# A decoder layer on one core: three tile pairs from plain to seven products, one of four opening pieces in one pass, the last column half in a bank of its own

## The chip, the cores and the metric

The kernel runs on one core of a Trainium2 chip. The metric is the device time of one execution in microseconds (us); less is better.

## The reference

One decoder layer, 512 tokens of 1024 features in float32, and three steps, each with a residual and a layer norm:

```python
def swiglu(x, w_gate, w_up, w_down):
    return (jax.nn.silu(x @ w_gate) * (x @ w_up)) @ w_down      # 1024 -> 2816 -> 1024
...
x = layer_norm(ALPHA * x + 0.5 * swiglu(x, ffn1_w_gate[l], ffn1_w_up[l], ffn1_w_down[l]), ln1_g[l], ln1_b[l])
proj = x @ w_in[l]                                               # 1024 -> 3072
...                                                              # gated recurrence (4 heads) and causal conv
mix = jnp.concatenate([o_a, o_b], axis=-1) @ w_out[l]
x = layer_norm(ALPHA * x + mix, ln2_g[l], ln2_b[l])
x = layer_norm(ALPHA * x + 0.5 * swiglu(x, ffn2_w_gate[l], ffn2_w_up[l], ffn2_w_down[l]), ln3_g[l], ln3_b[l])
```

## The kernel before

Every float32 operand of a product is split into a high and a low part (`split`): ScalarE casts the high part (L68), VectorE, or GpSimd for some weights of the mixing step, subtracts it from the raw value (L76). A product is then three matmuls, high by high, high by low and low by high (`mm3`, L194 to L196).

**Gate and up products.** The 2816 hidden columns of an FFN are 11 tile pairs f of 2 x 128 columns. For each there is a gate quad (s = 0) and an up quad (s = 1) of weights, one DMA of 1 MB each. A quad is taken in one of two ways. `plain` streams 512 tokens: 2 column tiles x 8 row tiles x 3 = 48 matmuls of 512 columns. `seven` cuts tokens, rows and columns in halves and needs seven half products instead of eight (`SEVEN`, `product`, L414): 7 x 4 x 3 = 84 matmuls of 256 columns, in the order p7, p1, p4, p5, p2, p6, p3. For it VectorE forms sums of weight quarters (L143, L149, L150) and splits three and a half 1024-element pieces instead of two; for the tokens it forms `x.sums()` (s1, s2, s3) and later `last_sum()` (s4). p4 adds into the PSUM area of p7, so ScalarE has to copy p7 out first (L434). The first `PLAIN` = 2 pairs of each FFN are plain, the other nine seven.

**Two seams.** The down product and the output product are made by `rows_out`: for the second half of the columns the last four weight units are kept, and the four token tiles are finished one after the other. Each is added to the residual (L333), its statistics taken (L334, L339), normalized (L221 and L343 on VectorE, the power on GpSimd at L222, then L347), transposed on TensorE (eight matmuls, L274 or L288), cast by ScalarE and its low part made by VectorE (L278 or L291). To keep TensorE busy while the last two tiles are normalized, the first four column products of the next step (`four_halved` before the mixing step, `begin` before the second FFN) run in token halves, t = 0 for tokens 0 to 255 first. They are 4 x 24 matmuls of 256 columns for t = 0, then as many for t = 1, which needs the transposes of the last tiles. `NORM_WAITS` says how much of this goes ahead of the transposes of tile 2 and of tile 3. The last tile's last unit is taken in two column halves of 256, both in one PSUM bank.

**Order.** TensorE's order is that of the code (`manual_schedule`); a scheduler orders the other engines. Each engine runs its queue in that order. The parts of weights lie in 6 slots (`parts`), the raw weights in 2 buffers (`raws`).

Of the kernel before, what the change touches and what calls it, by code (L numbers as in the profile page):

```python
# [17 lines left out]
P = 128  # L18
# [8 lines left out]
PLAIN = 2  # L27
# [22 lines left out]
NORM_WAITS = (1.3, 6.2)  # L50
# [3 lines left out]
def decoder_layer(ctx, tc, x_tok, x_q, w_first, vec, bcast, ng, w_gu1, w_d1, w_i, w_g, w_col, w_o, w_gu2, w_d2, out):  # L54
# [115 lines left out]
    def plan_quads(src, first):  # L170
        todo.extend(("plain" if f < PLAIN else "seven", src[f, s]) for f in range(first, NP) for s in range(2))

# [8 lines left out]
    plan_quads(w_gu1, 1)  # L181
# [8 lines left out]
    plan_quads(w_gu2, 0)  # L190
# [122 lines left out]
    def rows_out(ks, per, lhs, accs, factor, late, finish, follow=(), before=lambda u: None, then=lambda: None):  # L313
# [4 lines left out]
        n_units = len(ks) // per  # L318

        wide = [512] * (NT - 1) + [256]  # L320
        stats = [small.tile([P, 1024 // n, 6], F32, tag=f"stats{n}", name="stats") for n in wide]

        def part(acc, u, hi, lo, i, cols=slice(0, 512)):
            for j in range(per):
                n = per * u + j
                h, l = lhs(ks[n])
                mm3(acc[i][:, cols], h[:, i * P:(i + 1) * P], l[:, i * P:(i + 1) * P],
                    hi[:, j, cols], lo[:, j, cols], n == 0, n == len(ks) - 1, skip_group_check=wide[i] < 512)

        def add(acc, half, i, c):  # L330
            n = wide[i]
            z = xres[i][:, half * 512 + c:half * 512 + c + n]
            nc.vector.scalar_tensor_tensor(z, acc[i][:, c:c + n], factor, z, op0=ALU.mult, op1=ALU.add)  # L333
            nc.vector.bn_stats(stats[i][:, (half * 512 + c) // n, :], z)  # L334
# [16 lines left out]
        with tc.manual_schedule(engines={PE}):  # L351
            for u in range(n_units):
                before(u)
                hi, lo = unit()
                for i in range(NT):
                    part(acc, u, hi, lo, i)
        for i in range(NT):
            for c in range(0, 512, wide[i]):
                add(acc, 0, i, c)
        acc = [bank(b) for b in accs[1]]  # L360
        for u in range(n_units - late):
            hi, lo = unit()
            for i in range(NT):
                part(acc, u, hi, lo, i)
# [4 lines left out]
        with tc.manual_schedule(engines={PE}):  # L369
            left = deque()  # L370
            for i in range(NT):
                for n, (u, hi, lo) in enumerate(kept[:-1]):
                    part(acc, u, hi, lo, i)
# [6 lines left out]
                for c in range(0, 512, wide[i]):  # L380
                    add(acc, 1, i, c)
# [9 lines left out]
    def four_halved(pp, banks):  # L391
# [677 lines left out]
```

## Time and profile before

| | |
|---|---|
| median of 3 runs | 935.68 us (934.78 to 935.89) |
| profiled execution | 935.08 us, its span 933.1 us, 1.98 us around it |
| mean granted TensorE clock | 0.998 |
| TensorE (PE) busy | 923.2 us, 99% of the span |
| VectorE (DVE), ScalarE (ACT), GpSimd (POOL) busy | 72%, 41%, 13% |

A matmul's record is longer than its distance to the next, since matmuls are pipelined: what one costs in a dense stretch is the distance from start to start. Times in the rows are us from the start of the span.

### The profile page before, as it was taken

Reading aid. Unit: us, or ns where it says so; the run is one execution under the profiler, and the core shown is the slowest. Engines: PE = TensorE matmul, PEld = TensorE weight load, DVE = VectorE, ACT = ScalarE, POOL = GpSimd, SP = SyncE. Lnnn points to the kernel's source line nnn. Section 1 sums busy time; section 2 is a strip of 40 time slices with the busy share of each in tenths; the row PEclk is TensorE's granted clock in tenths of the full one; section 3 lists DMA queues with packets and bytes.
Section 4 is the critical chain, followed back from the end, with each engine's and each line's share of the span. In section 5 each row is a group of like instructions: output and inputs, shape, how many; then the busy total and the mean of one; then the engine's idle time right before and its main releaser. Section 6 shows DMA issues by size and latency. Waiting matters only on the chain.

```text
span 933.1 us, 14256 instructions
## 1 busy us (share of the span) xinstructions
PE 923.2 (99%) x5899; PEld 836.8 (90%) x5899; DVE 673.8 (72%) x953; ACT 384.1 (41%) x564; POOL 120.8 (13%) x142
## 2 busy tenths in 40 slices
PE   9999999999999999999999999999999999999996
PEld 6899999999888889888888888989999999988885
DVE  6978888887724265998898769948888887842317
ACT  5555445456412114414342714534545545721100
POOL 0000000000820014643462201000000000000001
PEclk9999999999999999999999999999999999999999
DMA  8522332324432212422130251122232222443302
GB/s 295 201 94 91 112 115 91 124 81 147 140 109 91 91 45 92 136 68 68 51 108 23 73 199 67 70 91 91 92 120 107 91 96 98 146 136 92 111 1 90
DMA packets 22464, 96.67 MB, mean 104 GB/s; under 512 B 2496, under 2 KB 3648, under 8 KB 17024
## 3 DMA queue, kind: packets, MB, share of 16 engines
q1 hardware_dynamic: 22320, 95.50, 30.6%
q8 instruction: 46, 0.75, 0.3%
q0 software_dynamic: 80, 0.26, 0.1%
q14 instruction: 18, 0.15, 0.1%
HBM read 93.66 MB, written 2.10 MB: 103 GB/s over the span
## 4 chain that ended last, share of the span: by engine, by line
PE 90%; DVE 4%; issue 3%; POOL 2%; DMA 1%; ACT 1%; DVEq 0%; POOLq 0%; ACTq 0%
PE bank L414 39%; PE bank L194 16%; PE bank L196 16%; PE bank L195 16%; DVE bank L771 2%; PE bank L849 1%; POOL wlo L76 1%; PE bank L274 0%; PE bank L288 0%; DMA raw<-w_g 0%; DMA xr<-x_q 0%; DVE diag L798 0%; DVE bl L954 0%; DVE m L906 0%; PE bank L920 0%
## 5 line engine op out<-in xcount | busy, mean ns | idle before, releaser
L68 ACT CAST whi<-raw 128x1024 fp32r<-128x1024 f32 (+2 forms) x172 | 172.9, 1010 | 307.3 <-PE bank L196 145.9
L76 DVE TENSOR_TENSOR wlo<-raw,whi 128x1024 fp32r<-128x1024 f32 (+2 forms) x150 | 173.4, 1164 | 174.1 <-ACT whi L68 174.0
L194 PE MATMUL bank<-whi,hp 128*128 128x512 f32 x324 | 125.9, 389 | 0.0
L196 PE MATMUL bank<-whi,hp 128*128 128x512 f32 x324 | 125.6, 388 | 0.0
L195 PE MATMUL bank<-wlo,hp 128*128 128x512 f32 x324 | 125.5, 387 | 0.0
L414 PE MATMUL bank<-ah,whi 128*128 128x256 f32 x432 | 122.5, 283 | 0.0
L414 PE MATMUL bank<-bl,whi 128*128 128x256 f32 x432 | 122.3, 283 | 0.0
L414 PE MATMUL bank<-ah,wlo 128*128 128x256 f32 x432 | 122.2, 283 | 0.0
L414 PE MATMUL bank<-al,whi 128*128 128x256 f32 x432 | 122.2, 283 | 0.0
L414 PE MATMUL bank<-bh,whi 128*128 128x256 f32 x432 | 122.2, 283 | 0.0
L414 PE MATMUL bank<-bh,wlo 128*128 128x256 f32 x432 | 122.2, 283 | 0.0
L771 DVE SCALAR_TENSOR_TENSOR bank<-u,vecs,bank 128x512 f32<-128x512 f32 x120 | 81.5, 750 | 3.8 <-ACT bank L766 3.6
L414 PEld LDWEIGHTS bank<-ah,whi 128*128 128x128 f32 x432 | 82.9, 192 | 0.2
L414 PEld LDWEIGHTS bank<-bh,whi 128*128 128x128 f32 x432 | 82.9, 192 | 0.1
L414 PEld LDWEIGHTS bank<-bl,whi 128*128 128x128 f32 x432 | 82.9, 192 | 0.1
L414 PEld LDWEIGHTS bank<-bh,wlo 128*128 128x128 f32 x432 | 82.9, 192 | 0.0
L414 PEld LDWEIGHTS bank<-al,whi 128*128 128x128 f32 x432 | 82.9, 192 | 0.0
L414 PEld LDWEIGHTS bank<-ah,wlo 128*128 128x128 f32 x432 | 82.9, 192 | 0.0
L222 POOL TENSOR_TENSOR rstd<-rstd,negh 128x1 f32<-128x1 f32 (+1 forms) x18 | 16.8, 935 | 509.4 <-DVE rstd L221 509.4
L76 POOL TENSOR_TENSOR wlo<-raw,whi 128x256 fp32r<-128x256 f32 x88 | 69.4, 821 | 61.1 <-ACT whi L68 59.1
L196 PEld LDWEIGHTS bank<-whi,hp 128*128 128x128 f32 x324 | 60.9, 188 | 12.8
L195 PEld LDWEIGHTS bank<-wlo,hp 128*128 128x128 f32 x324 | 60.9, 188 | 12.7
(210 smaller groups left out, 1911.2 us busy)
## 6 DMA issues: line engine op xcount, KB each, us to landing
raw<-w_gu SPq DMA_DIRECT2D x42, 1024.0 KB, 4.8
raw<-w_d SPq DMA_DIRECT2D x44, 512.0 KB, 3.5
raw<-w_col SPq DMA_DIRECT2D x16, 512.0 KB, 3.5
raw<-w_o SPq DMA_DIRECT2D x8, 512.0 KB, 3.5
xres<-x_tok SPq DMA_DIRECT2D x4, 512.0 KB, 7.8
gb<-bcast SPq DMA_DIRECT2D x4, 512.0 KB, 4.5
raw<-w_i SPq DMA_DIRECT2D x4, 512.0 KB, 3.4
raw<-w_g SPq DMA_DIRECT2D x4, 512.0 KB, 3.3
```

Of the source, the lines that this page charges most:

```text
L68: nc.scalar.copy(hi, raw)
L76: engine.tensor_tensor(lo[..., sl], raw[..., sl], hi.bitcast(F32)[..., sl], op=ALU.subtract)
L194: nc.tensor.matmul(ps, lhsT=lh, rhs=rh, start=first, stop=False, **kw)
L195: nc.tensor.matmul(ps, lhsT=lh, rhs=rl, start=False, stop=False, **kw)
L196: nc.tensor.matmul(ps, lhsT=ll, rhs=rh, start=False, stop=last, **kw)
L222: nc.gpsimd.tensor_tensor(r, r, negh.broadcast_to([P, n]) if n > 1 else negh, op=ALU.pow)
L414: nc.tensor.matmul(ps, lhsT=l[:, k, :], rhs=r[:, k, :], start=first and k == 0 and j == 0, stop=k == 3 and j == 2, skip_group_check=True)
L771: nc.vector.scalar_tensor_tensor(accs[n], us[n][:, j:j + T], vecs[:, w:w + 1], accs[n], op0=ALU.mult, op1=ALU.add)
L849: nc.tensor.matmul(ps[0:P - m, g, 0:64].rearrange("p (b m) -> p b m", m=m), lhsT=k[:, h, g * P:(g + 1) * P - m], rhs=halved(q, m, 1)[:, h, ...
```

## The change

1. `PLAIN` becomes a set of (f, s) for each FFN: `PLAINS`. In the first FFN the up quad of pair 1, in the second FFN the gate and the up quad of pair 1 are made with seven products. `last_sum` follows the first seven product, wherever it is.
2. In `four_halved` and `begin` the fourth piece is no longer cut in token halves: it runs whole, after the t = 1 halves of the other three. `NORM_WAITS` goes from 1.3 to 1.2.
3. In `rows_out` the last tile's last column half of 256 goes to the bank of the tile before it, as an accumulation of its own; what the older bank holds of these columns is added to the residual separately.

```diff
-PLAIN = 2
+PLAINS = ((0, 0), (0, 1), (1, 0)), ((0, 0), (0, 1))
...
-NORM_WAITS = (1.3, 6.2)
+NORM_WAITS = (1.2, 6.2)
...
-        todo.extend(("plain" if f < PLAIN else "seven", src[f, s]) for f in range(first, NP) for s in range(2))
+        todo.extend(("plain" if (f, s) in plain else "seven", src[f, s]) for f in range(first, NP) for s in range(2))
...
-                for c in range(0, 512, wide[i]):
-                    part(acc, *kept[-1], i, slice(c, c + wide[i]))
-                if i == NT - 1:
+                if i < NT - 1:
+                    add(acc[i], i, 512, 1024)
+                else:
+                    part(acc[i][:, 0:256], *kept[-1], i, slice(0, 256))
+                    add(acc[i][:, 256:512], i, 768, 1024, False)
+                    add(acc[i][:, 0:256], i, 512, 768)
+                    ps = bank(accs[1][i - 1], 256)
+                    part(ps, *kept[-1], i, slice(256, 512), True)
                     ahead(SLOTS)
-                for c in range(0, 512, wide[i]):
-                    add(acc, 1, i, c)
+                    add(ps, i, 768, 1024)
                 norm(i)
...
-            for ps, (hi, lo) in zip(pp, us):
+            for ps, (hi, lo) in zip(pp[:3], us):
                 for k in range(NK):
                     mm3(ps[:, sl], hi[:, k, :], lo[:, k, :], xh[:, k, sl], xl[:, k, sl], k == 0, k == NK - 1)
                     yield MM3 / 2
+        for k in range(NK):
+            mm3(pp[3], *(w[:, k, :] for w in us[3]), xh[:, k, :], xl[:, k, :], k == 0, k == NK - 1)
+            yield MM3
...
-                for f in range(PLAIN, NP):
+                first = True
+                for f in range(1, NP):
                     h.append(h_of(f))
                     for s in range(2):
...
+                        if (f, s) in plains:
+                            got = [bank(i, 2, H) for i in bb]
+                            run(plain(got, x, [w]))
+                            plain_gate_up(s, got)
+                            continue
```

`begin` is changed as `four_halved` is. The lines of the kernel after stand about one lower at the top (L69 for L68, L77 for L76) and up to 13 lower further on.

What the change does to the queues of the other engines is seen in the order in which instructions stand. First, ScalarE at the start of the first FFN: before, its queue from the exponential of the bounds (`e`) to the first copy out of a seven product; `h` is the hidden tile, `whi` and `w2hi` are high parts of weights.

```order
L620 ACTIVATE e_308<-e_308 128x8
L510 ACT_TABLE_LOAD
L510 ACTIVATE h_323<-bank0_171 128x512
L510 ACTIVATE h_323<-bank1_172 128x512
...
L510 ACTIVATE h_323<-bank4_350 128x512
L68 CAST w2hi_467<-raw_455 128x512
L510 ACTIVATE h_323<-bank5_351 128x512
...
L434 COPY h_454<-bank2_478 128x256
L434 COPY h_454<-bank0_477 128x256
```

The same place of ScalarE's queue after:

```order
L633 ACTIVATE e_320<-e_320 128x8
L69 CAST whi_394<-raw_392 128x1024
L69 CAST whi_400<-t13_398 128x1024
L69 CAST ah_83<-xr_88 128x1024
L520 ACT_TABLE_LOAD
L520 ACTIVATE h_335<-bank0_171 128x512
L520 ACTIVATE h_335<-bank1_172 128x512
L520 ACTIVATE h_335<-bank4_340 128x512
L520 ACTIVATE h_335<-bank6_341 128x512
L441 COPY work_414<-bank7_416 128x256
L441 COPY work_414<-bank5_415 128x256
```

The table load and all four activations now stand right ahead of the first copy, that of p7 out of bank 7, and behind casts for the seven products. On VectorE, after, these are the rows that stand from the first weights to `lb`, for the element of the bounds on which the table load waits (`al`, `bl`, `wlo`, `w2lo` are low parts, `t13` and `raw` sums of weight quarters):

```order
L77 TENSOR_TENSOR wlo_274<-raw_271,whi_273 128x1024
L77 TENSOR_TENSOR wlo_278<-raw_271,whi_277 128x1024
L77 TENSOR_TENSOR bl_86<-xr_87,bh_85 128x1024
L77 TENSOR_TENSOR wlo_294<-raw_291,whi_293 128x1024
L144 TENSOR_TENSOR t13_297<-raw_291 128x1024
L77 TENSOR_TENSOR w2lo_304<-raw_291,w2hi_303 128x512
L150 TENSOR_TENSOR raw_291<-raw_291,t13_297 128x512
L77 TENSOR_TENSOR wlo_300<-t13_297,whi_299 128x1024
L151 TENSOR_TENSOR raw_291<-raw_291 128x512
...
L144 TENSOR_TENSOR t13_398<-raw_392 128x1024
L77 TENSOR_TENSOR wlo_310<-raw_291,whi_309 128x1024
...
L77 TENSOR_TENSOR wlo_395<-raw_392,whi_394 128x1024
...
L77 TENSOR_TENSOR wlo_401<-t13_398,whi_400 128x1024
L636 TENSOR_TENSOR lb_80<-e_320,mx_319 128x4
```

Before, only the first four of these and one more `wlo` stood ahead of `lb`. Second, GpSimd at the first seam: the powers of the four tiles' norms (`rstd`) and the low parts of the mixing step's first weights, before.

```order
L222 TENSOR_TENSOR rstd_3330<-rstd_3330,negh_78 128x1
L222 TENSOR_TENSOR rstd_3417<-rstd_3417,negh_78 128x1
L76 TENSOR_TENSOR wlo_3395<-raw_3393,whi_3394 128x256 x4
L76 TENSOR_TENSOR wlo_3404<-raw_3402,whi_3403 128x256 x4
L752 MEMSET u_3687 128x30
```

After, the power of tile 3 stands behind four of the subtractions:

```order
L223 TENSOR_TENSOR rstd_3385<-rstd_3385,negh_78 128x1
L77 TENSOR_TENSOR wlo_3454<-raw_3452,whi_3453 128x256 x4
L223 TENSOR_TENSOR rstd_3474<-rstd_3474,negh_78 128x1
L77 TENSOR_TENSOR wlo_3463<-raw_3461,whi_3462 128x256 x4
L765 MEMSET u_3720 128x30
```

Third, VectorE at the second seam, from the norm of tile 3 (`xres3`) to the low parts of its transposes (`al`), before:

```order
L343 SCALAR_TENSOR_TENSOR xres3_76<-xres3_76,mv_5383,m1_3673 128x512 x2
L347 SCALAR_TENSOR_TENSOR xres3_76<-xres3_76,rstd_5385,m1_3673 128x512 x2
L143 TENSOR_TENSOR t13_5658<-raw_5652 128x1024
L76 TENSOR_TENSOR w2lo_5665<-raw_5652,w2hi_5664 128x512
L291 TENSOR_TENSOR al_5175<-bank6_5487,ah_5174 128x4x128
L291 TENSOR_TENSOR al_5175<-bank7_5495,ah_5174 128x4x128
```

And after:

```order
L151 TENSOR_TENSOR raw_5405<-raw_5405 128x512
L331 SCALAR_TENSOR_TENSOR xres3_76<-bank4_5388,xres3_76 128x256
...
L339 BN_AGGR mv_5429<-stats_5013 128x2
L144 TENSOR_TENSOR t13_5658<-raw_5652 128x1024
L222 TENSOR_SCALAR rstd_5431<-mv_5429 128x1
L343 SCALAR_TENSOR_TENSOR xres3_76<-xres3_76,mv_5429,m1_3706 128x512 x2
L347 SCALAR_TENSOR_TENSOR xres3_76<-xres3_76,rstd_5431,m1_3706 128x512 x2
L77 TENSOR_TENSOR w2lo_5665<-raw_5652,w2hi_5664 128x512
L150 TENSOR_TENSOR raw_5652<-raw_5652,t13_5658 128x512
L292 TENSOR_TENSOR al_5207<-bank6_5530,ah_5206 128x4x128
L292 TENSOR_TENSOR al_5207<-bank7_5538,ah_5206 128x4x128
```

A 512-element sum of weights and the third add now stand ahead of tile 3's statistics, a 1024-element sum stands inside its norm, and two 512-element rows instead of one between the norm and `al`.

## Rows read from the trace of the kernel before

**Rows 1.** The page, parts 1 and 2: busy time, and the granted TensorE clock.

```profile
PE 923.2 (99%) x5899; PEld 836.8 (90%) x5899; DVE 673.8 (72%) x953; ACT 384.1 (41%) x564; POOL 120.8 (13%) x142
...
PEclk9999999999999999999999999999999999999999
```

**Rows 2.** What TensorE waited for: us in total, times, longest.

```profile
PE bank L849 <- DVE qk L835: 0.3, 1, 0.3
PE bank L910 <- DVE m L906: 0.3, 1, 0.3
```

**Rows 3.** The chain that ended last: start, us, what.

```profile
49.13 181.67 PE bank L414 x1512
```

**Rows 4.** Timeline, TensorE, second seam and pair 1: start, us, what.

```profile
586.96 0.36 PE L194 MATMUL bank<-ah,whi 128*128 128x256 f32 x1
...
601.07 0.40 PE L194 MATMUL bank<-ah,whi 128*128 128x512 f32 x1
...
622.85 0.28 PE L414 MATMUL bank<-bh,whi 128*128 128x256 f32 x1
```

**Rows 5.** Timeline, VectorE, start of the first FFN.

```profile
25.39 2.35 DVE L76 TENSOR_TENSOR wlo<-raw,whi 128x1024 fp32r<-128x1024 f32 x2
...
31.99 0.16 DVE L623 TENSOR_TENSOR lb<-e,mx 128x4 f32<-128x4 f32 x1
...
37.88 0.68 DVE L76 TENSOR_TENSOR w2lo<-raw,w2hi 128x512 fp32r<-128x512 f32 x1
38.48 0.69 DVE L149 TENSOR_TENSOR raw<-raw,t 128x512 f32<-128x512 f32 x1
```

**Rows 6.** Timeline, ScalarE and TensorE, start of the first FFN.

```profile
32.25 1.28 ACT L510 ACT_TABLE_LOAD   x1 [0.71 <-DVE lb L623]
33.55 1.09 ACT L510 ACTIVATE h<-bank 128x512 f32<-128x512 f32 x2
...
27.21 0.39 PE L194 MATMUL bank<-ah,whi 128*128 128x512 f32 x1
```

**Rows 7.** Timeline, VectorE, first seam.

```profile
352.19 2.35 DVE L76 TENSOR_TENSOR wlo<-raw,whi 128x1024 fp32r<-128x1024 f32 x2
...
358.59 2.38 DVE L347 SCALAR_TENSOR_TENSOR xres<-xres,rstd,gb 128x512 f32<-128x512 f32 x2
363.95 1.29 DVE L278 TENSOR_TENSOR xl<-bank,xh 128x512 fp32r<-128x512 f32 x2 [2.98 <-ACT xh L277]
```

**Rows 8.** Timeline, ScalarE, GpSimd and TensorE, first seam.

```profile
357.10 1.05 ACT L68 CAST whi<-raw 128x1024 fp32r<-128x1024 f32 x1 [0.76 <-DMA raw<-w_col]
...
357.43 0.98 POOL L222 TENSOR_TENSOR rstd<-rstd,negh 128x1 f32<-128x1 f32 x1 [7.93 <-DVE rstd L221]
358.38 6.66 POOL L76 TENSOR_TENSOR wlo<-raw,whi 128x256 fp32r<-128x256 f32 x8
...
362.70 1.04 PE L274 MATMUL bank<-ident,xres 128*128 128x128 f32 x8
...
363.70 0.28 PE L195 MATMUL bank<-xl,whi 128*128 128x256 f32 x1
```

**Rows 9.** Timeline, VectorE and TensorE, second seam.

```profile
570.02 0.69 DVE L333 SCALAR_TENSOR_TENSOR xres<-bank,xres 128x512 f32<-128x512 f32 x1 [0.74 <-PE bank L196]
...
575.64 4.62 DVE L76 TENSOR_TENSOR wlo<-raw,whi 128x1024 fp32r<-128x1024 f32 x4
...
584.19 1.41 DVE L347 SCALAR_TENSOR_TENSOR xres<-xres,rstd,m 128x512 f32<-128x512 f32 x2
...
586.17 1.03 PE L288 MATMUL bank<-ident,xres 128*128 128x128 f32 x8
```

**Rows 10.** Timeline, VectorE, the last tile's adds at the end.

```profile
925.22 0.76 DVE L333 SCALAR_TENSOR_TENSOR xres<-bank,xres 128x256 f32<-128x256 f32 x2 [1.10 <-PE bank L196]
```

**Rows 11.** Last stretch: us, busy PE, PEld, DVE, ACT, POOL, granted clock, DMA.

```profile
929.00:933.10 4.10, 0.00 (x0) 0.00 (x0) 0.76 (x2) 0.00 (x0) 0.00 (x0) 0.54 0.33 128
```

**Rows 12.** The page, part 6: weight loads of gate and up, median us to landing.

```profile
raw<-w_gu SPq DMA_DIRECT2D x42, 1024.0 KB, 4.8
```

More of the change, by code (lines that the diff above doesn't have):

```diff
@@ L318, in rows_out, with part @@
         n_units = len(ks) // per
-        wide = [512] * (NT - 1) + [256]
-        stats = [small.tile([P, 1024 // n, 6], F32, tag=f"stats{n}", name="stats") for n in wide]
-        def part(acc, u, hi, lo, i, cols=slice(0, 512)):
+        stats = [small.tile([P, n, 6], F32, tag=f"stats{n}", name="stats") for n in [2] * (NT - 1) + [4]]
+        def part(ps, u, hi, lo, i, cols=slice(0, 512), fresh=False):
             for j in range(per):
@@ L326, in part, with add @@
                 h, l = lhs(ks[n])
[L327 to L334, printed above, removed]
+                mm3(ps, h[:, i * P:(i + 1) * P], l[:, i * P:(i + 1) * P],
+                    hi[:, j, cols], lo[:, j, cols], n == 0 or fresh and j == 0, n == len(ks) - 1)
+        def add(ps, i, a, b, last=True):
+            z = xres[i][:, a:b]
+            nc.vector.scalar_tensor_tensor(z, ps, factor, z, op0=ALU.mult, op1=ALU.add)
+            n = 256 if i == NT - 1 else 512
+            for c in range(a, b, n) if last else ():
+                nc.vector.bn_stats(stats[i][:, c // n, :], xres[i][:, c:c + n])
         def norm(i):
@@ L355, in rows_out @@
                 for i in range(NT):
-                    part(acc, u, hi, lo, i)
+                    part(acc[i], u, hi, lo, i)
         for i in range(NT):
-            for c in range(0, 512, wide[i]):
-                add(acc, 0, i, c)
+            add(acc[i], i, 0, 512)
         acc = [bank(b) for b in accs[1]]
@@ L363, in rows_out @@
             for i in range(NT):
-                part(acc, u, hi, lo, i)
+                part(acc[i], u, hi, lo, i)
         then()
@@ L471, in begin @@
         for t in range(2):
-            for ps, (w, l) in zip(begun, ((w, l) for w in ws for l in range(2))):
+            for ps, (w, l) in zip(begun[:3], ((w, l) for w in ws for l in range(2))):
                 for k in range(NK):
@@ L476, in begin, with ffn @@
                     yield MM3 / 2
+        for k in range(NK):
+            mm3(begun[3], *tile_parts(ws[1], 1, k), *x.rows(k // 4, k % 4), k == 0, k == NK - 1)
+            yield MM3
         ahead(AHEAD)
-    def ffn(x, begun, gb_i, finish, follow=(), then=lambda: None, later=lambda: None):
+    def ffn(x, begun, plains, gb_i, finish, follow=(), then=lambda: None, later=lambda: None):
         with tc.tile_pool(name="ffn", bufs=1) as fp:
@@ L504, in gate_up, with plain_gate_up @@
                     nc.vector.tensor_tensor(g[:, 1:4], g[:, 1:4], pr.work[:, 1:4], op=ALU.mult)
-            def plain_gate_up(banks):
-                h.append(h_of(len(h)))
+            def plain_gate_up(s, banks):
                 g = h[-1].rearrange("p (l t) c -> p l t c", l=2)
                 for l in range(2):
-                    nc.scalar.activation(g[:, l], banks[l], AF.Silu)
-                for l in range(2):
-                    nc.vector.tensor_tensor(g[:, l], banks[2 + l], g[:, l], op=ALU.mult)
+                    if s == 0:
+                        nc.scalar.activation(g[:, l], banks[l], AF.Silu)
+                    else:
+                        nc.vector.tensor_tensor(g[:, l], banks[l], g[:, l], op=ALU.mult)
             with tc.manual_schedule(engines={PE}):
-                plain_gate_up(begun)
-                for f in range(1, PLAIN):
-                    ahead(4)
-                    ws = [unit_now() for _ in range(2)]
-                    ahead(3)
-                    got = [bank(i, 2, H) for i in chain(*zip(*PAIR_BANKS[f % 2]))]
-                    run(plain(got, x, ws))
-                    plain_gate_up(got)
-                for f in range(PLAIN, NP):
+                h.append(h_of(0))
+                for s in range(2):
+                    plain_gate_up(s, begun[2 * s:2 * s + 2])
+                first = True
+                for f in range(1, NP):
                     h.append(h_of(f))
@@ L664, in next_operand @@
         operand[:] = make()
[L666 removed]
+    ffn(x1, begun, PLAINS[0], 0, after(transposed, 4), four_halved(conv_first, (6, 7, 0, 1)),
         lambda: next_operand(plain_operand), later)
```

20 lines of the change are left out of this document (10 added, 10 removed).

## The prediction

> **What bounds the kernel now.** The page first: TensorE is busy 923.2 of 933.1 us, at full granted clock in all 40 slices [rows 1]. Busy records overlap, so the waits come next: after its start TensorE waits twice, 0.3 us each, both in the mixing step [rows 2]. Then the chain: one of its pieces is 181.67 us of 1512 half-product matmuls without a break [rows 3]. So the kernel is the sum of TensorE's start distances, plus some 5 us at the start and 8 us behind the last matmul. Every other engine is late only where TensorE, whose order is fixed, has to wait for it. So two sums are needed: the TensorE work that goes, and the waits that come.
>
> **What goes.** A 256-column matmul of seven products costs 181.67 / 1512 = 0.1201 us [rows 3]. The 96 plain matmuls of pair 1 run from 601.07 to 622.85: 0.2269 each [rows 4]. A plain quad is 48 x 0.2269 = 10.89 us, a seven quad 84 x 0.1201 = 10.09. Three quads change: 3 x 0.80 = 2.4 us. The token halves of `begin` have 117 matmuls between 586.96 and 601.07, 0.1206 each [rows 4], so a halved piece is 48 x 0.1206 = 5.79 us and a whole one 24 x 0.2269 = 5.45; two pieces change: 0.7 us. At the end the two adds of the last tile, 0.76 us for both, start only at 925.22, after the whole bank [rows 10]. With the last half in another bank, two adds can run while its six matmuls (0.72 us) do, and one is left: 0.3 us less. Together 3.4 us.
>
> The Trainium skill (TensorE: Matmul & The Clock Gate, Back-to-back issue gap) gives 262 cycles for 256 columns and 518 for 512 at 2.4 GHz: 109.2 and 215.8 ns. The rows show 120.1 and 226.9 ns in a dense stream with a weight load for each matmul, so the measurement decides. By the page the three quads would give 3 x (10.36 - 9.17) = 3.6 us, the pieces 0.1, and the sum of what goes would be 4.0 us instead of 3.4.
>
> **What comes, first: the start of the first FFN.** The seven products begin after the plain gate quad of pair 1, at 27.21 + 10.89 = 38.10 [rows 6], no longer at 48.99 after both plain quads. p4 is third and due at 38.10 + 2 x 1.44 = 40.98. It adds to the bank that ScalarE must first copy p7 out of. In ScalarE's new order this copy stands behind the table load and four activations, and the load waits for `lb` on VectorE, as now (0.71 us, ended by lb) [rows 6]. VectorE now reaches `lb` at 31.99 [rows 5]. After, from 25.39 on, its queue holds nine 1024-element rows, of 1.135 us (the difference of four in 4.62 and two in 2.35 [rows 5, 9]), and four of 512, of 0.60 [rows 5], before `lb`: 10.2 + 2.4 = 12.6 us. Seven small ones of the bounds and waits for ScalarE's casts in between I put at 1.3 us. That makes `lb` 39.3, the load 39.4 to 40.7 (1.28), four activations of 0.55 (two in 1.09 [rows 6]) to 42.9, the copy, of half as many elements, some 0.3 to 43.2: p4 is 2.2 us late. Bounds: without the 1.3, 0.9 us; with another cast of 1.05 exposed, 3.2. The operands themselves are in time: the slots of the parts are free (first-stage weights by 27.2, the gate quad's by 38.1), and t1/t3 are split by 33.5.
>
> **Second: the first seam.** Now the transposes of tile 3 run at 362.70, and the 21 matmuls of t = 0 that are left hide its casts. After, 4 + 20 steps take exactly the 24 of three pieces. The transposes come one step earlier, 362.34, and t = 1 follows at once. Even with no other delay, its second matmul must wait for the first low part: now the transposes start at 362.70, the two low parts end at 363.95 + 1.29, so the first at 364.6, against 363.70 for that matmul [rows 7, 8]: 1.0 us. On top comes GpSimd: the power of tile 3 is now behind four subtractions of the first `w_col` unit. Their cast ends at 358.15 [rows 8], unchanged, since that load waits for a buffer that VectorE frees with the first row of [rows 7], which stays first. Four subtractions at 0.73 to 0.83 us (eight in 6.66 [rows 8]), the power 0.98: done at 362.1 to 362.5 instead of 358.4. L347 takes 1.41 for two [rows 9] or 2.38 beside GpSimd [rows 7], so the norm is done at 363.6 to 364.8, the first low part at 364.3 to 365.5, against a need at 363.34. TensorE waits 1.0 to 2.2 us; I take 2.0, since GpSimd is at its next subtractions then, as in rows 7 and 8.
>
> **Third: the second seam.** Here GpSimd is free, VectorE is not. Now the norm of tile 3 ends at 584.19 + 1.41 = 585.60, 0.57 before the transposes at 586.17 [rows 9]. The first seven quad moves into this stretch, and VectorE gets before that norm one 512-element sum (0.60), a third add (0.35) and a 1024-element sum (1.14) more: 2.1 us. It comes to the four splits at 575.64 some 0.3 us later: three rows (2.3 us) for the same quad stand earlier, where the queue now has gaps for TensorE of 0.74 [rows 9] and about 1.1 before it. So the norm ends at 588.0. The transposes, due at 585.81, end at 588.6. Then two 512-element rows (1.2 us) stand before the first low part (0.65): 589.9, against a need at 585.81 + 1.0 = 586.8. TensorE waits 3.1 us. Bounds: 1.0 as at the first seam, and 4.0 if the 1024-element sum, first in its queue, waits for its load: its buffer is free at about 579.3, and 4.8 us [rows 12] put the landing at 584.1, just when VectorE comes to it. The seven products themselves, at about 604 instead of 623, have their sums: s3 is split about 599.5.
>
> The third add and the fresh bank cost nothing before the end: the bank of tile 2 was read 24 matmuls earlier. In the mixing step TensorE is later by the first seam's wait while the convolution starts as early as now, so the two waits of 0.3 [rows 2] should go: 0.3 us gained, between 0.6 gained and 1 lost to a changed order on VectorE.
>
> **Sum.** -3.4 + 2.2 + 2.0 + 3.1 - 0.3 = +3.6 us on the profiled execution's 935.08: 938.7. The median is 0.6 higher than that execution; halfway between is 939.0. By bounds: the seams and the start at their least, 0.9 + 1.0 + 1.0, give 934.2; at their most 3.2 + 2.2 + 4.0 and 1 lost, 942.1.
>
> **Rivals.** (a) *The new waits shrink to what no order can hide*: the seams cost 1.0 each and the start nothing, because `lb` is earlier than my ledger has it. -3.4 + 2.0 - 0.3 = -1.7: 933.7, no change that counts. For it: VectorE's idle time, 28%. Against: the three orders, whose rows have fixed lengths. (b) *Faster*: TensorE finds all operands, and only its work counts: 935.4 - 3.4 = 932.0, 0.37% less. It needs all waits together below 1.5 us, and the first low part after the last transposes alone costs 1.0 at each seam; for it speaks that TensorE now waits nowhere. (c) *The clock falls at a seam.* TensorE's clock was still full 4 us after the last matmul and fell near 929.3: the mean from 929.0 on is 0.54 [rows 11]. A wait of 3.1 us is shorter than these 4. If it fell, the price per seam would be that of matmuls at half the clock until it rises, some 1.5 us as 7 matmuls of 0.23 at twice their time: 940.5 to 942. The Trainium skill (TensorE: Matmul & The Clock Gate, The HAM clock gate) says that the clock is throttled by default and that an idle stretch brings it back to half; by that rule the seam could cost more than its wait, and the end of this trace agrees that idle time lowers it. (d) *A load late at the second seam*, as above, 1 to 2 us more: 940 to 941.
>
> **How the numbers follow.** My forecast, slower by 2 to 6 us, has a chance of 0.65, its own range 937.3 to 941.2; (a) 0.17, (b) 0.07, (c) 0.06, (d) 0.05. About 0.2% (1.9 us) is what a measurement of this kernel can tell from no change, so below 933.8 is faster and above 937.5 slower. (a) is split: 0.05 of it lies below 933.8. Faster 0.12, same 0.12, slower 0.76. Leaving out (b), that part of (a) and the far end of (c), the range is 933.8 to 941.6.
>
> **What would show it.** In the trace after: a wait of TensorE of about 2 us near 41 us, ended by ScalarE's copy; waits at both seams, first at the transposes of tile 3, then at the low part behind them, about 2 and 3 us; 84 matmuls in 10.09 us for the three quads; the final adds ending 0.3 us sooner after the last matmul. The forecast is wrong if `lb` is done before 37.5, if GpSimd's power of tile 3 ends before 360, or if the norm at the second seam ends within 0.5 us of the transposes' time.

## The result and the profile after

The changed kernel takes 941.00 us in the median of 6 runs (939.45 to 943.22), the kernel before 935.55 (934.78 to 936.52): a ratio of 1.006, with a 95% interval of 1.005 to 1.007. It is slower by 5.45 us. The profiled execution took 941.29 us with a span of 939.3, 6.2 more than before. First the page after, parts 1 and 2:

```profile
PE 923.8 (98%) x5959; PEld 839.5 (89%) x5959; DVE 693.5 (74%) x980; ACT 391.7 (42%) x579; POOL 119.3 (13%) x142
...
PEclk9999999999999999999999999999999999999998
```

Busy time of TensorE is nearly what it was [rows 1], although it has less to do; the rest of the time must be in waits. What TensorE waited for (us in total, times, longest):

```profile
PE bank L421 <- ACT work L441: 2.4, 2, 2.0
PE bank L289 <- DVE xres L347: 1.5, 1, 1.5
...
PE bank L275 <- issue: 0.9, 1, 0.9
PE bank L196 <- DVE al L292: 0.7, 1, 0.7
PE bank L275 <- DVE xres L347: 0.6, 1, 0.6
```

Before, TensorE waited twice for 0.3 us after its start [rows 2]. The stages, by the start times of TensorE's matmuls in the two profiled executions, show where the difference lies (T(0) is the first transpose of a seam):

| stage, us | before | after | difference | predicted |
|---|---|---|---|---|
| start of the span to the first down product | 230.64 | 234.13 | +3.49 | +1.4 |
| down product of the first FFN, to T(0) | 110.74 | 110.75 | 0.0 | 0 |
| first seam: T(0) to the end of the four pieces | 36.22 | 38.12 | +1.90 | +1.7 |
| mixing step and output product, to T(0) | 187.18 | 186.80 | -0.38 | -0.3 |
| second seam: T(0) to the end of the four pieces | 36.29 | 39.13 | +2.84 | +2.8 |
| rest of gate and up, second FFN | 203.44 | 202.10 | -1.34 | -1.6 |
| down product, to the start of the last matmul | 120.39 | 120.39 | 0.0 | 0 |
| from there to the end | 8.19 | 7.85 | -0.34 | -0.3 |

The start of the first FFN, on the timeline of TensorE, VectorE and ScalarE:

```profile
38.07 0.28 PE L421 MATMUL bank<-bh,whi 128*128 128x256 f32 x1
...
39.16 0.15 DVE L636 TENSOR_TENSOR lb<-e,mx 128x4 f32<-128x4 f32 x1
...
39.40 1.28 ACT L520 ACT_TABLE_LOAD   x1 [0.86 <-DVE lb L636]
40.69 2.07 ACT L520 ACTIVATE h<-bank 128x512 f32<-128x512 f32 x4
42.61 0.68 ACT L441 COPY work<-bank 128x256 f32<-128x256 f32 x2
...
43.07 0.50 PE L421 MATMUL bank<-ah,whi 128*128 128x256 f32 x1 [1.98 <-ACT work L441]
```

`lb` ends on VectorE, the table load follows, then the four activations, then the copy of p7. The third product, p4, starts at 43.07 instead of 40.94: a wait of 2.13 us (waits at a matmul are given here as the start distance less the usual 0.12). Behind this wait the windows show the granted clock (us, then busy time of PE, PEld, DVE, ACT and POOL, the granted clock, the DMA share, GB/s):

```profile
41.00:43.00 2.00, 0.10 (x1) 0.00 (x0) 2.00 (x4) 2.00 (x6) 0.00 (x0) 1.00 0.00 0
43.00:44.00 1.00, 0.93 (x4) 0.93 (x5) 1.00 (x2) 0.74 (x3) 0.00 (x0) 0.59 0.00 0
44.00:45.00 1.00, 1.00 (x7) 1.00 (x6) 1.00 (x2) 0.60 (x1) 0.00 (x0) 0.50 0.00 0
...
46.00:47.00 1.00, 1.00 (x8) 1.00 (x8) 0.46 (x1) 0.00 (x0) 0.00 (x0) 0.70 0.30 66
47.00:48.00 1.00, 1.00 (x11) 1.00 (x10) 0.00 (x0) 0.37 (x1) 0.00 (x0) 1.00 0.76 221
```

From 43 to 46.5 the clock is at half, and the matmuls there stand 0.213 us apart instead of 0.120. So the first stage is -0.80 for the quad, +2.13 for the wait, 0.61 for a wait at the last pair of tiles, and 1.55 that is left for the clock (16 matmuls 0.093 us longer each are 1.5). The wait at the last pair stands in the chain that ended last (start, us, what):

```profile
219.88 4.31 DMA raw<-w_d
...
224.30 1.05 ACT whi L69
...
226.41 0.27 ACT work L441
...
226.73 1.34 PE bank L421 x9
```

A load of down weights lands, its cast stands ahead of the activation on ScalarE, and the copy (`work`) that TensorE waits for stands behind both. The same happens once in the second FFN (0.30 us). The two seams on the timeline, of GpSimd, VectorE and TensorE, the first:

```profile
361.75 3.29 POOL L77 TENSOR_TENSOR wlo<-raw,whi 128x256 fp32r<-128x256 f32 x4 [8.76 <-ACT whi L69]
364.99 0.55 POOL L223 TENSOR_TENSOR rstd<-rstd,negh 128x1 f32<-128x1 f32 x1
...
365.58 2.35 DVE L347 SCALAR_TENSOR_TENSOR xres<-xres,rstd,gb 128x512 f32<-128x512 f32 x2 [2.54 <-POOL rstd L223]
...
366.89 0.63 PE L275 MATMUL bank<-ident,xres 128*128 128x128 f32 x4 [0.90 <-issue]
368.07 0.63 PE L275 MATMUL bank<-ident,xres 128*128 128x128 f32 x4 [0.55 <-DVE xres L347]
```

and the second:

```profile
589.06 1.23 DVE L144 TENSOR_TENSOR t<-raw 128x1024 f32<-128x1024 f32 x1
...
591.59 1.41 DVE L347 SCALAR_TENSOR_TENSOR xres<-xres,rstd,m 128x512 f32<-128x512 f32 x2
592.91 0.68 DVE L77 TENSOR_TENSOR w2lo<-raw,w2hi 128x512 fp32r<-128x512 f32 x1
...
594.12 1.28 DVE L292 TENSOR_TENSOR al<-bank,ah 128x512 fp32r<-128x512 f32 x2
...
592.48 1.29 PE L289 MATMUL bank<-ident,xres 128*128 128x128 f32 x8 [1.49 <-DVE xres L347]
...
594.85 0.39 PE L196 MATMUL bank<-al,whi 128*128 128x256 f32 x1 [0.69 <-DVE al L292]
```

At the first the power of tile 3 stands behind four subtractions, so the second half of its norm ends late and the transposes come in two halves. At the second the norm of tile 3 ends at 593.0 and TensorE waits 1.65 us for the transposes and 0.95 for the low part. At the end, the last matmul starts at 931.42 and three adds (before: two, [rows 10]) begin before it:

```profile
931.02 1.14 DVE L331 SCALAR_TENSOR_TENSOR xres<-bank,xres 128x256 f32<-128x256 f32 x3 [0.39 <-PE bank L197]
```

They end 0.74 us after the start of the last matmul; before, the two end 1.08 us after it.

The granted clock is on record for each of the six runs as a mean: 0.994 or 0.995 in the three longest (941.29 to 943.22), 0.997 to 0.999 in the three shortest (939.45 to 940.72). So the clock fell in some executions and probably not in others, and the profiled one is of the first kind.

### The profile page after: what moved, and what is told of

It is laid out like the page before. It is cut to its first block, busy times and chain, and to the rows that moved or that the text cites. A ratio compares the mean times of both kernels' runs of the same rounds, so it can differ in the third digit from the quotient of the medians.

```text
span 939.3 us, 14422 instructions
## 1 busy us (share of the span) xinstructions
PE 923.8 (98%) x5959; PEld 839.5 (89%) x5959; DVE 693.5 (74%) x980; ACT 391.7 (42%) x579; POOL 119.3 (13%) x142
## 4 chain that ended last, share of the span: by engine, by line
PE 89%; DVE 5%; DMA 2%; ACT 2%; issue 1%; SPq 0%; POOL 0%; DVEq 0%; ACTq 0%
PE bank L421 40%; PE bank L195 15%; PE bank L196 15%; PE bank L197 15%; PE bank L862 2%; DVE wlo L77 1%; DMA xr<-x_q 1%; DMA raw<-w_d 1%; PE bank L906 0%; ACT whi L69 0%; PE bank L844 0%; PE bank L872 0%; DVE t L144 0%; PE bank L820 0%; PE bank L275 0%
## 5 line engine op out<-in xcount | busy, mean ns | idle before, releaser
L69 ACT CAST whi<-raw 128x1024 fp32r<-128x1024 f32 (+2 forms) x172 | 173.0, 1010 | 309.6 <-PE bank L197 144.8
L77 DVE TENSOR_TENSOR wlo<-raw,whi 128x1024 fp32r<-128x1024 f32 (+2 forms) x150 | 173.7, 1163 | 172.4 <-ACT whi L69 170.2
L421 PE MATMUL bank<-ah,whi 128*128 128x256 f32 x468 | 133.3, 285 | 2.6 <-ACT work L441 2.4
L421 PE MATMUL bank<-al,whi 128*128 128x256 f32 x468 | 133.0, 284 | 0.0
L421 PE MATMUL bank<-ah,wlo 128*128 128x256 f32 x468 | 133.0, 284 | 0.0
L421 PE MATMUL bank<-bh,whi 128*128 128x256 f32 x468 | 132.7, 283 | 0.0
L421 PE MATMUL bank<-bl,whi 128*128 128x256 f32 x468 | 132.6, 283 | 0.0
L421 PE MATMUL bank<-bh,wlo 128*128 128x256 f32 x468 | 132.6, 283 | 0.0
L421 PEld LDWEIGHTS bank<-ah,whi 128*128 128x128 f32 x468 | 90.3, 193 | 3.2 <-ACT work L441 3.2
L421 PEld LDWEIGHTS bank<-ah,wlo 128*128 128x128 f32 x468 | 90.4, 193 | 0.0
L421 PEld LDWEIGHTS bank<-al,whi 128*128 128x128 f32 x468 | 90.4, 193 | 0.0
L421 PEld LDWEIGHTS bank<-bh,whi 128*128 128x128 f32 x468 | 90.1, 193 | 0.1
L77 POOL TENSOR_TENSOR wlo<-raw,whi 128x256 fp32r<-128x256 f32 x88 | 68.6, 811 | 70.0 <-ACT whi L69 69.8
```

The lines of the kernel that those rows point to most:

```text
L69: nc.scalar.copy(hi, raw)
L77: engine.tensor_tensor(lo[..., sl], raw[..., sl], hi.bitcast(F32)[..., sl], op=ALU.subtract)
L421: nc.tensor.matmul(ps, lhsT=l[:, k, :], rhs=r[:, k, :], start=first and k == 0 and j == 0, stop=k == 3 and j == 2, skip_group_check=True)
```

## The experiments

Four questions: what each part of the change costs by itself, whether the waits have the causes named, whether the clock follows the wait, and whether a version is faster than both kernels. Each run is compared with runs of the kernel before on the same chip (medians 935.57, 935.22 and 935.28 us in the three sets). Stage times are read as in the table above, each from one profiled execution. Two stages differ between profiles where an edit does not reach: the first by up to 0.6 us (the run with two quads of the second FFN alone), the mixing step by up to 0.6 (the run with the up quad alone).

**One part alone, the up quad of the first FFN.** The kernel before in the form of the changed code, with

```diff
-PLAINS = ((0, 0), (0, 1), (1, 0), (1, 1)), ((0, 0), (0, 1), (1, 0), (1, 1))
+PLAINS = ((0, 0), (0, 1), (1, 0)), ((0, 0), (0, 1), (1, 0), (1, 1))
```

> The kernel before with one part of the change alone: the up quad of pair 1 of the first FFN by seven products. Theory (the wait is ScalarE's queue: the copy of p7 stands behind the table load and four activations, and the load waits for lb): the quad gives back 0.8 us, TensorE waits 2.1 us at its third product, 0.6 us are lost at the last pair, and 1.5 us more in executions in which the clock falls behind the wait: 937.5 to 939.1. Rival (the wait at the start comes from the other parts too, the quad alone is a gain): 934.8.

Measured: 937.52 us, ratio 1.0026 (1.0015 to 1.0037). The seven times stand in two groups, 936.93 to 937.52 (four) and 939.05 to 939.49 (three). The profiled execution is of the upper group, and in it TensorE waits 2.64 us at the third product and then has half the clock, as this window shows:

```profile
44.00:45.00 1.00, 1.00 (x6) 1.00 (x6) 1.00 (x2) 0.89 (x1) 0.00 (x0) 0.50 0.00 0
```

The theory holds: the part alone is a loss. Of its terms, the 0.6 us at the last pair are 0.2 in this profile, and the mixing step, which this part does not touch, takes 0.63 more. The groups are 1.9 us apart. That the lower one is the executions without the fall is likely: the mean granted clock is 0.997 to 0.999 there and 0.996 to 0.997 in the upper group, but none of the lower was profiled.

**One part alone, the two quads of the second FFN.**

```diff
-PLAINS = ((0, 0), (0, 1), (1, 0), (1, 1)), ((0, 0), (0, 1), (1, 0), (1, 1))
+PLAINS = ((0, 0), (0, 1), (1, 0), (1, 1)), ((0, 0), (0, 1))
```

> The kernel before with one part alone: gate and up quad of pair 1 of the second FFN by seven products. Theory (VectorE's rows for these quads make the norm of tile 3 late only where the cover behind it is short too): the quads give back 1.6, the last pair loses 0.3, and the second seam 0.3, since one sum of 0.6 us more stands ahead of a norm that had 0.57 us to spare: 934.6. Rival (these rows alone make the norm of tile 3 some 1.8 us late, with or without the whole piece): 936.2.

Measured: 935.34 us, ratio 0.9997 (0.9988 to 1.0006), between the two forecasts. The seam takes 36.29 us as before, so the rival is wrong: the extra rows do not make the norm late by themselves. The theory's 0.3 us for the seam is not there either. The gain of 1.6 us shows in the trace as 0.6, since TensorE waits 1.03 us at the last pair, at 795.7, behind a load of down weights of 4.65 us.

**One part alone, whole pieces.** Part 2 of the change, on the kernel before: the fourth piece whole and `NORM_WAITS` at 1.2.

> The kernel before with one part alone: the fourth piece whole at both seams. Theory (a whole piece gains 0.34 and uncovers 1.0 us of cast and low part; the rest of the two seam waits comes from the order on GpSimd and VectorE that other parts cause): 0.7 lost at each seam, 0.4 gained in the mixing step: 936.5. Rival (the seam waits of the changed kernel, 2.2 and 3.2 us, are the price of the missing cover alone): 939.9.

Measured: 937.23 us, ratio 1.0020 (1.0012 to 1.0029). Each seam takes 0.83 us more (37.05 and 37.13 for 36.22 and 36.29), so a wait of some 1.2 us against a gain of 0.34; the mixing step takes 0.31 more instead of 0.4 less, which is most of the 0.7 us by which the median is above the theory's 936.5. The power of tile 3 stands ahead of the subtractions here, at 357.30, as before [rows 8]. At the second seam a row ahead of the low parts waits for its load, on VectorE's timeline:

```profile
587.33 1.22 DVE L144 TENSOR_TENSOR t<-raw 128x1024 f32<-128x1024 f32 x1 [0.59 <-DMA raw<-w_gu]
588.47 1.28 DVE L292 TENSOR_TENSOR al<-bank,ah 128x512 fp32r<-128x512 f32 x2
```

So the price of the missing cover is near the theory's 0.7 for each seam, far from the 1.9 and 2.84 of the changed kernel.

**One part alone, the bank of the last column half.** Part 3 of the change, on the kernel before, in all three steps.

> The kernel before with one part alone: the last column half of the last tile in a bank of its own, in all three places where the last tile is finished. Theory (this part, not the whole piece, is what puts four subtractions ahead of the power of tile 3 on GpSimd): the transposes of tile 3 at the first seam run 1.8 us late in two halves, the end gains 0.3, the mixing step 0.3: 936.7. Rival (the fresh bank costs nothing before the end, as the prediction had it): 935.3.

Measured: 936.56 us, ratio 1.0013 (1.0004 to 1.0021). GpSimd's timeline at the first seam:

```profile
358.27 3.45 POOL L77 TENSOR_TENSOR wlo<-raw,whi 128x256 fp32r<-128x256 f32 x4 [8.71 <-ACT whi L69]
361.68 0.54 POOL L223 TENSOR_TENSOR rstd<-rstd,negh 128x1 f32<-128x1 f32 x1
```

The power is behind four subtractions, as in the changed kernel, with neither seven products nor whole pieces. The seam takes 37.80 us, 1.58 more; the mixing step 0.59 more, where 0.3 less was expected; the second seam nothing more; the end 0.33 less. The theory holds for the seam and the end, and the rival, a sentence of the prediction, falls. Which line of part 3 moves the power (the third add, or the adds' new place between the matmuls) was not tried apart.

The four parts alone add up to 1.95 - 0.23 + 1.66 + 0.99 = 4.4 us, of 5.45. In the profiled executions the second seam is where they are not additive: 0.00, 0.84 and 0.00 for the last three parts, 2.84 for all.

**The bounds early.** The changed kernel, with the token sums moved behind the load of the bounds and the rows up to `lb`:

```diff
-        ahead(2)
-        x1.sums()
-        ahead(3)
-        make_identity(nc, ident)
-        nc.gpsimd.memset(negh, -0.5)
         nc.sync.dma_start(out=vecs, in_=vec)
...
         nc.vector.tensor_tensor(lb, e[:, 0, :], mx, op=ALU.mult)
         nc.vector.tensor_scalar(oml, lb, -1.0, 1.0, op0=ALU.mult, op1=ALU.add)
+        ahead(2)
+        x1.sums()
+        ahead(3)
+        make_identity(nc, ident)
+        nc.gpsimd.memset(negh, -0.5)
```

> The changed kernel with one edit: the bounds (the small rows that end in lb) are issued ahead of the sums of the tokens. Theory (the wait near 41 us is the table load behind lb on ScalarE, and the clock falls because of that wait): lb is done before 30 us, no wait at the third product and no fall of the clock there: 941.0 less 2.1 less about 1.0 that the falls cost in the median: 937.5 to 938.2. Rival (the casts and splits of the first seven quad are late too, so that the table load is only the last of several): about 1 us of the wait stays, 939.5.

Measured: 938.68 us (938.17 to 940.90), ratio 1.0036 (1.0023 to 1.0050), 0.5 us above the theory's range and 0.8 below the rival. The wait at 41 us is gone and the clock stays full there, which shows that the wait was for `lb`. Two things came instead. TensorE waits 1.35 us at the third product of another quad, at 61 us, and VectorE is now busy 23.89 of the 24 us from 38 to 62. And in the profiled execution, the slowest of the five, the clock is at half after the second seam, whose two waits are those of the changed kernel; its windows:

```profile
593.00:594.00 1.00, 1.00 (x5) 1.00 (x6) 0.37 (x1) 0.98 (x2) 0.00 (x0) 0.50 0.06 16
...
597.00:598.00 1.00, 1.00 (x10) 1.00 (x10) 1.00 (x2) 0.99 (x2) 0.00 (x0) 1.00 0.00 0
```

The seam takes 40.57 us with it, 1.44 more than the 39.13 of the changed kernel, in whose profile the clock stayed full there.

**A longer wait.** The first experiment, with one copy more on ScalarE ahead of that of p7:

```diff
                             plain_gate_up(s, got)
+                            if not gb_i and f == 1:
+                                spare = work_tile()
+                                for _ in range(1):
+                                    nc.scalar.copy(spare.rearrange("p a b -> p (a b)"), h[-1].rearrange("p a b -> p (a b)"))
                             continue
```

> The up quad of pair 1 of the first FFN by seven products alone, with one copy of 1024 elements more on ScalarE (to a spare tile, which nothing reads) ahead of the copy of p7, and so a cast of 1.05 us behind it too: the wait grows from 2.3 to about 4.2 us. Theory (the clock falls after a wait of this place if it is long enough; 2.3 us are near the edge, which is why the times of this part alone stood in two groups): it falls in every execution, one group of times near 940.6. Rival (whether it falls is chance and not the length): two groups again, near 939.0 and 940.9.

Measured: 941.17 us (939.91 to 941.74), ratio 1.0061 (1.0049 to 1.0074). The wait is 4.47 us, and the clock falls behind it, as in this window:

```profile
47.00:48.00 1.00, 1.00 (x7) 1.00 (x7) 0.00 (x0) 0.00 (x0) 0.00 (x0) 0.50 0.39 82
```

The five times do not stand in two groups, which speaks for the theory; they spread over 1.8 us, about the distance of the two groups of the first experiment, so this is not settled. Their mean granted clocks, 0.994 to 0.997, lean to a fall in each. That length alone does not decide, two later runs show: a wait of 2.47 us without a fall in the last, a fall after 1.95 us in the one with a unit on GpSimd.

**The order mended.** The changed kernel with the bounds early, and with part 3 only where no step follows:

```diff
+                    if follow:
+                        part(acc[i][:, 256:512], *kept[-1], i, slice(256, 512))
+                        ahead(SLOTS)
+                        add(acc[i][:, 0:256], i, 512, 768)
+                        add(acc[i][:, 256:512], i, 768, 1024)
+                    else:
                         add(acc[i][:, 256:512], i, 768, 1024, False)
...
```

> The changed kernel with the bounds early, and with the bank of its own for the last column half only at the end of the kernel, where no step follows. Theory (the two seams are late by the order on GpSimd and VectorE that the last part brought, and the whole piece itself costs 0.8 a seam): start 0.8 gained, seams 0.8 each, the two quads of the second FFN 1.3 gained, mixing step 0.3 lost, end 0.3 gained: 935.3, the power of tile 3 ahead of the subtractions again. Rival (at the second seam the rows of the seven products make the norm late whatever the order): 2.8 there, 937.3.

Measured: 935.86 us, ratio 1.0005 (0.9996 to 1.0014), 5.1 us less than the changed kernel and 0.6 above the theory. On GpSimd's timeline the power stands ahead of the subtractions again:

```profile
357.70 0.99 POOL L223 TENSOR_TENSOR rstd<-rstd,negh 128x1 f32<-128x1 f32 x1 [7.82 <-DVE rstd L222]
```

The seams take 0.83 and 1.02 us more than before, not 1.90 and 2.84. Whole pieces and seven products are both in this kernel, so the rival is wrong: at the second seam it took the order of part 3 as well to bring the 2.84 (with the bounds early alone, both waits of this seam stayed). Still 0.84 us are waited for at 61 us, and 0.7 at the last pairs.

**The parts that should gain.** As the last, but with all four pieces in halves and `NORM_WAITS` at 1.3, as before.

> The three quads by seven products with the bounds early, the bank of its own at the end of the kernel alone, all four pieces in halves as before. Theory (the seven products gain once nothing stands ahead of the copy of p7, and the seams are those of before): 0.8 gained at the start, 0.2 to 1.6 in the second FFN, 0.3 at the end: 932.9 to 934.3. Rival (the loads of the down weights set the end of the gate and up products, so that what the quads give back is waited for at the last pair): 935.3.

Measured: 934.59 us, ratio 0.9991 (0.9982 to 1.0000): 0.1% less than before at an interval that ends at no change, 0.3 us above the theory's range and below the rival's 935.3. What is gained comes from the second FFN, 1.6 us, and from the end, 0.34. The first FFN takes longer than before: TensorE waits 0.84 us at 61.7 and 0.92 at 223.9, against 0.80 for the quad, and 0.6 went at the first matmuls of this profile, which the edit does not reach. The second wait is behind a load of down weights of 4.67 us. VectorE is the reason for the first: the cast ahead of ScalarE's activations and copy waits for it, and its busy time is the third number of the window:

```profile
60.24 1.05 ACT L69 CAST whi<-raw 128x1024 fp32r<-128x1024 f32 x1 [0.64 <-DVE raw L151]
...
25.00:62.00 37.00, 36.93 (x254) 34.35 (x252) 36.74 (x47) 22.86 (x32) 0.00 (x0) 1.00 0.40 142
```

It is busy 36.74 of 37 us there; before, 31.55 in the same window. The start of the first FFN has hardly room for one more quad with its sums and its splits.

**Only the second FFN and the end.** The kernel before with its two quads by seven products, and the bank only where no step follows.

> The kernel before with the two quads of the second FFN by seven products and the bank of its own at the end of the kernel alone. Theory (the first FFN's quad gives nothing, because VectorE is full there until 62 us and the wait only moves; these two parts are all that gains): 1.6 less for the quads, up to 1.0 of it waited for at the last pair where the load of the third down unit takes 4.6 us instead of 3.5, 0.35 less at the end: 933.4 to 934.4. Rival (the last pair always waits, so the quads give nothing): 935.0.

Measured: 935.02 us (933.79 to 935.79), ratio 0.9994 (0.9985 to 1.0003). The median is the rival's, but that the last pair always waits is not so: in the profile of the run before, TensorE waits for nothing in the second FFN. In this one TensorE waits 1.83 us at the last pair; the chain that ended last:

```profile
786.78 5.45 DMA raw<-w_d
...
792.31 1.06 ACT whi L69
...
793.39 1.23 DVE wlo L77
...
795.78 0.38 ACT h L509
```

The load takes 5.45 us, where the four loads at this place take 3.4 to 3.6 in the kernel before. It is issued at 786.78 instead of 788.49, earlier by what the quads save, so it does not fall behind TensorE by that; it is 1.94 us longer, and that is waited for, nearly in full. In the profile of the run before the same load takes 3.44 us, and nothing is waited for. Why it is longer here is not known.

**One unit on GpSimd.** As the last, with this for the third unit of the down weights, in both FFNs:

```diff
-        split(raw, hi, lo, lo_engine)
+        if hi_engine is None:
+            split(raw, hi, lo, lo_engine)
+        else:
+            hi_engine.tensor_copy(hi, raw)
+            rest(lo, raw, hi, lo_engine)
...
+    todo.append(("unit", w_d1[0, 2], tok, nc.gpsimd, nc.gpsimd))
```

> As the run before it, and in both FFNs the third unit of the down weights is cast and subtracted on GpSimd, so that no cast that waits for its load stands ahead of the activation and the copies of the last pair on ScalarE. Theory (the wait at the last pair is the load of that unit, behind which the activation and the copy of p7 or p1 queue): no wait there, 933.3 in all executions. Rival (the copies wait for VectorE's rows of the last pair, or GpSimd slows VectorE): the wait stays, 934.0 to 934.6.

Measured: 939.48 us, ratio 1.0042 (1.0030 to 1.0055). The theory falls: the waits are 2.34 us at the last pair of the first FFN and 1.95 at that of the second. The first is new, brought by the edit. The chain there goes through GpSimd's low part of the third unit and the load that starts behind it:

```profile
222.61 3.87 POOL wlo L77 x4
...
226.49 3.50 DMA raw<-w_d
```

The cast of that load stands ahead of TensorE's copy on ScalarE. In the second FFN it is the second unit whose load (4.73 us) is late, and its low part stands on VectorE ahead of the rows that the activation waits for. Behind this wait the clock falls as well, to half from 800.9 to 804.3. GpSimd's cast makes the wait longer, on the timelines of GpSimd and VectorE:

```profile
795.24 1.88 POOL L95 CAST whi<-raw 128x1024 fp32r<-128x1024 f32 x1 [208.39 <-DMA raw<-w_d]
...
796.13 1.26 DVE L456 TENSOR_TENSOR h<-h 128x256 f32<-128x256 f32 x1
```

That sum of 256 elements takes 0.42 us in the run before it. The Trainium skill (Perfetto Trace Analysis, Optimizing Scalar/DVE Operations) warns that work moved from VectorE to GpSimd may not help, because the two share a read port; this row agrees, with 1.26 for 0.42 us.

**The first quads relieved.** The kernel of all the parts that should gain, with the low part of the first pieces of three quads of the first FFN on GpSimd:

```diff
+        def helped(self):
+            self.both(("b11", "b21"), self.raw[:, 0:4:3, :], nc.gpsimd)
+            self.inner()
...
+    for i in (1, 2, 3):
+        todo[i] = ("helped", todo[i][1])
```

> All three quads by seven products, bounds early, bank of its own at the end alone, and the low part of the first pieces of three quads of the first FFN on GpSimd instead of VectorE. Theory (VectorE has too much between 25 and 62 us once the wait at 41 is gone, which moved 0.8 to 1.4 us of it to 61): three rows of 1.14 us less, no wait at 61, 0.85 less than without: 933.8. Rival (GpSimd's 8 short rows for a piece are too late, or slow VectorE beside them): 934.6 or more.

Measured: 934.50 us, ratio 0.9990 (0.9981 to 0.9999), the lowest of all, but by 0.1 us only against the same kernel without it. GpSimd takes long, by its timeline:

```profile
29.05 7.61 POOL L77 TENSOR_TENSOR wlo<-raw,whi 128x128 fp32r<-128x128 f32 x8 [27.68 <-ACT whi L69]
```

0.95 us for each of 8 rows, where VectorE needs 1.14 for all. The wait at 61 shrinks to 0.31, and two new ones appear, 0.86 at 43.7 and 0.62 at 51.9; the 0.88 at the last pair of the first FFN stay.

**All mended.** Both edits on GpSimd together, with all that the last kernel has.

> The two edits on GpSimd together, with all three quads by seven products, bounds early, bank of its own at the end alone, all pieces in halves. Theory (each wait has one cause and the causes are apart): 2.4 less for the quads and 0.35 at the end, no wait at 41, 61 or at the last pairs: 932.6. Rival (one of the waits stays): 933.3 to 934.0.

Measured: 938.41 us, ratio 1.0031 (1.0020 to 1.0043). The waits of both edits add up (1.09, 0.62, 0.30, then 2.47 and 0.85 at the last pairs); the theory that no wait is left falls with that of the third unit.

## Why the prediction was right, and where it was not

**The sign and the terms of the sum.** The forecast was 939.0 with a range to 941.6; 941.0 is in it, on the far side. The sum by stages was +3.6 against +6.2 of the two profiled executions, and all but the first stage agree within 0.3 us. The three waits that the sum has were near the size forecast: 2.13 us at the start for 2.2, and at the seams, with the 0.34 of a whole piece added to the differences, 2.24 for 2.0 and 3.18 for 3.1. Their causes are shown by the runs that take them away (bounds early, the order mended) or have one alone (part 3). The norm of tile 3 at the second seam was forecast for 588.0 in the times of before; TensorE came to this seam 5.02 us later, which makes 593.0, and it ended at 593.0.

**Where luck helped.** The ledger of the start had `lb` at 39.3 and p4 at 43.2: they came at 39.3 and 43.07. But three errors cancel in it. Ten rows of 1024 and three of 512 elements stand before `lb`, as the order ahead of the prediction has them, not nine and four: 0.5 us more. VectorE began them at 25.64 and not at 25.39. And the small rows and waits for casts took 0.5 us, not 1.3. In the mixing step 0.37 us were gained, near the 0.3 forecast, but one of the two waits that should go stayed; the runs of one part alone took up to 0.63 more there without a reason that was found. That the median is inside the range is owed to the range's width, since costs of 2.5 us, below, are in no term of the sum. (The least of its bounds adds up to 934.3, not 934.2.)

**What goes** was sized right too: 0.80 for the quad, 0.34 at the end; in the second FFN 1.6, of which 0.30 was waited for again.

**The step that was wrong** is the sentence that the third add and the fresh bank cost nothing before the end. By itself this part costs 1.0 us in the median; in its profiled execution 1.58 at the first seam and 0.59 in the mixing step, against 0.33 gained at the end. The 0.59 need not be its own, since the up quad alone shows 0.63 there. It puts GpSimd's power behind four subtractions, which the prediction saw in the order and charged to the seam without asking which part had brought it. Since it priced the waits of the whole change, the sum was still right; as an account of which part costs what it was not. The whole piece, which it blamed, costs 0.83 a seam.

**The second seam**, 3.1 us by the sum, is the price of three parts together: none of them alone costs more than 0.84 there, and without the order of part 3 the other two cost 1.02.

**What was missing** is 2.6 us: 1.55 of the clock at the start, 0.61 and 0.30 at the two last pairs, the rest small. Rival (c) had the fall and the price (1.5), but placed it at the seams alone, with the argument that 3.1 us is shorter than the 4 of [rows 11]. It fell after 2.1 us at the start, and in another run at the second seam. The Trainium skill (TensorE: Matmul & The Clock Gate, Part 1: The HAM clock gate) says that an idle TensorE goes back to half the clock; the runs agree, with a granted clock of 0.50 behind waits of 2.13, 2.64 and 1.95 us. But there was no fall after 2.34 and 2.47 us. The wait at the last pairs was not thought of: the loads behind it took 4.31 and 4.05 us in this profile, where the same loads took 3.39 and 3.58 in that of before. Why is open.

**Rivals (a) and (b)** needed the start's wait and the seams at their least. Taking away the causes (bounds early, part 3 at the end alone) brings 935.86, so (a) is near the mended kernel's mechanism and not this one's, and even there its 933.7 is 2.2 us too low, since a wait at 61 us and those at the last pairs stay. The lowest medians, 934.59 and 934.50, are of kernels with all pieces in halves and part 3 at the end alone; 0.1% is at the edge of what these runs can tell from no change. Rival (d), a late load at the second seam, was not seen in the changed kernel; with whole pieces alone it was, with 0.59 us.

Open is what decides in which executions the clock falls. That the two groups of times of the first experiment are it is likely by their granted clocks, but not shown by a profile of each.

## What to carry to other kernels

When one engine is busy for 99% of the span, work taken from it pays only as far as the queues that feed it have time to spare at that place: the quad of the first FFN gave back 0.8 us of TensorE, but VectorE was then busy five us more in a window of 37, of which it was already busy for 31.6. After any edit to a scheduled kernel, compare the order on the engines that the edit does not touch, and try each part alone: the part that looked free moved one short row on GpSimd and cost more than it gained. A wait of about two us on TensorE has to be priced with the clock behind it, some 1.5 us in the executions in which it falls.

## What was not expected of the hardware

- The granted clock fell to 0.50 for about 3.5 us after a wait of 2.13 us (changed kernel), 2.64 and 4.47, after one of 1.95 (a unit on GpSimd, 797.6 to 799.7), and after the two waits of the second seam in one profile and not in another with the same waits. It did not fall after 2.47 us in the last run, nor after 2.34 us at 229 us in the run with one unit on GpSimd, the same execution in which it fell after 1.95. The windows of that run:

```profile
230.00:231.00 1.00, 0.00 (x0) 0.00 (x0) 0.00 (x0) 0.93 (x1) 0.00 (x0) 1.00 0.77 315
231.00:232.00 1.00, 0.56 (x4) 0.56 (x5) 0.85 (x1) 1.00 (x3) 0.00 (x0) 1.00 0.07 29
232.00:233.00 1.00, 1.00 (x11) 1.00 (x10) 1.00 (x4) 1.00 (x2) 0.00 (x0) 1.00 0.00 0
...
801.00:802.00 1.00, 1.00 (x6) 1.00 (x6) 0.80 (x1) 0.60 (x1) 0.00 (x0) 0.50 0.54 131
```

- Loads of the same 512 KB at the same place, the last pair of the second FFN, took 3.4 to 5.45 us from one run's profile to another's.
- A sum of 256 elements on VectorE took 1.26 instead of 0.42 us beside a cast on GpSimd.
